# Output weights of the second layer split one stage earlier and held in DRAM, and squares added up by VectorE after a transpose

## The chip, the cores and the metric

The kernel runs on one core of a Trainium2 chip. Its five engines are TensorE (PE in the profile; PEld is its weight load), VectorE (DVE), ScalarE (ACT), GpSimd (POOL) and SyncE (SP, which only issues DMAs here). The metric is device time in microseconds (us): the median of the runs of one program, 617.97 us for the kernel before (3 runs, 617.78 to 618.43).

## The reference

An encoder of two layers works on 256 positions of width 1024. A layer is a mixer and a feed-forward:

```python
h = rms_norm(x, n1); proj = h @ w_in_l                 # 1024 -> 2560
# q, k, v of three groups of heads (width 64): 4 neighbourhood, 6 dilated, 6 grouped-query heads
mix = concatenate([rms_norm(out_a, og[:256]), rms_norm(out_d, og[256:640]), rms_norm(out_c, og[640:])])
x = x + mix @ w_out_l                                  # 1024 -> 1024
h = rms_norm(x, n2); g, u = split(h @ w_gu, 2)         # 1024 -> 2 x 2816
x = x + (gelu(conv(g)) * u) @ w_dn                     # 2816 -> 1024
```

Everything is float32. Each of the three groups of heads has a norm of its own ahead of the output projection: the squares of a group's outputs are added over the group's width, position by position.

## The kernel before

**Arithmetic.** A float32 product is made of three fast ones. Each weight is split into a high part, rounded to the type float32r, and a low part, the rest; each activation likewise. `mm3` (L610) multiplies high by high, high by low and low by high.

**Weights** come in units (`units_of`, L544). A layer has 51: 12 of the projection w_in, 6 of w_out (L70: two halves of columns for each of three groups; four units of 3 x 512 columns per partition and two of 2 x 512), 11 each of gate, up and down. `load` (L561) issues one DMA per unit on SP's queue into one of four raw tiles. `split` (L584) makes the two parts in chunks, mostly of 512 columns: ScalarE copies to the high part, VectorE subtracts that from the raw values for the low part. There are two high and two low tiles, so a unit's split can begin only when the matmuls of the unit two before are done. `unit` (L599) takes the next unit and asks for the splits and loads ahead of it.

**The mixer** of a layer (L789 to L1225) normalises and transposes x, projects, and then runs 16 heads in the order dilated, grouped-query, neighbourhood: scores, softmax, transpose of the probabilities, product with the values. `Weave` (L665) puts the matmuls of the projections, and then those of the first four output units (`out_projections`, L826), between the steps of the heads. For each pair of heads `mixed` (L1032) writes the two parts of the outputs into `mixT_hi` and `mixT_lo`, and has the squares made on ScalarE and added on GpSimd. When a group's heads are done, `group_rstd` (L1047) adds those squares over the partitions: on TensorE, two matmuls of the squares with a column of ones, each of which the chip executes as two; VectorE copies the two result columns, and GpSimd works out the factor (`rstd_of`, L615: two instructions). The output projection's sum is then scaled by that factor and added to x on VectorE (L842). After the last group, the fifth and the sixth output unit remain (L1221 to L1225). x is transposed in two halves for the feed-forward (`split_T`, L623), the second of them between the gate unit's matmuls (L1249).

**The feed-forward** has 11 steps. Each takes a gate unit and an up unit (`half_up`, L1234) and a down unit (`down`, L1308). In steps 2 to 4 of layer 0 some tables for layer 1 are made (L1323 to L1330).

**Order.** Nothing is issued as it is written. `Plan` (L220) records every operation with an estimated duration (`cost`, L414), and `order` (L301) lists them again: always the one next that can start first by these estimates, and among equals the one of the lowest rank. `later(n)` adds n to the rank. `emit` (L406) then issues each in this order, so that nearly all instructions have line L411 in the profile and are told apart by their tiles: `wp_raw`, `wp_hi` and `wp_lo` are weights, `act_hT` is the transposed normalised x, `act_mixT` are the heads' outputs, `act_sqm` their squares, `const_x` is x, `psa` and `psw` are PSUM. Every engine then executes its list strictly in order.

Of the kernel before, what the change touches and what calls it, by code (L numbers as in the profile page):

```python
# [29 lines left out]
DEPTH = 2  # L30
# [6 lines left out]
UNIT = 2048  # L37
# [4 lines left out]
RAWS, PARTS, AHEAD, CHUNK = 4, 2, 2, 512  # L42
# [10 lines left out]

SUM_ACT, SCALE_ACT = ("dq", "dk", "cq"), ("dk",)

SPLIT_LATER, TURN_LATER, MIX_LATER, PREP_LATER = 50, 100, 100, 30
GKV_W = H_GKV * HD
_CD = 3 * H_NA * HD
_WD = H_DIL * HD
# [10 lines left out]
OUT_ORDER = [(0, 0), (0, 512), (1, 0), (1, 512), (2, 0), (2, 512)]  # L70

FFN = [("G", 0), ("U", 0)]
# [147 lines left out]
class Plan:  # L220
# [5 lines left out]
    def pool(self, real, name, bufs, space=bass.MemoryType.SB):  # L226
        return PlanPool(self, real, name, bufs, space)
# [226 lines left out]
def encoder_kernel(  # L454
# [21 lines left out]
    nc = Plan(tc)  # L476
# [3 lines left out]
    const = pool("const", 1)  # L480
    wp = pool("wp", 3)
    act = pool("act", 2)
# [3 lines left out]
    dram = pool("dram", 1, space=bass.MemoryType.DRAM)  # L486
# [7 lines left out]
    ident = const.tile([P, P], F32, tag="ident", name="ident")  # L494
# [7 lines left out]
    def load_x(c, n, by):  # L502
        cs = slice(c * P, (c + n) * P)
        by.dma_start(xs[:, :, cs], xv[:, :, cs])
# [23 lines left out]
    minus_half = const.tile([P, 32], F32, tag="mh", name="minus_half")  # L528
    nc.gpsimd.memset(minus_half, -0.5)

    ones = const.tile([P, 1], F32, tag="ones", name="ones")
    nc.gpsimd.memset(ones, 1.0)

    vown, vkv = (
        [const.tile([P, NT, 2 * n + 1, HD], F32R, tag=f"v{n}{i}", name=f"v{n}{i}") for i in range(2)]
# [8 lines left out]
    def units_of(l):  # L544

        for c0, width in PROJ:
            per = 4 if width * 8 > UNIT else 8
            for k0 in range(0, KD, per):
                yield rows(w_in[l], k0, per, c0, width)
        for gi, c0 in OUT_ORDER:  # L550
            yield rows(w_out[l], *OUTP[gi], c0, 512)
        for kind, s in FFN:
            if kind == "D":
                yield rows(w_down[l], 2 * s, 2, 0, D)
            else:
                yield rows(w_gate_up[l], 0, KD, (D_FF if kind == "U" else 0) + s * 2 * P, 2 * P)

    views = [v for l in range(DEPTH) for v in units_of(l)]
    raws, parts, taken = [], [], [0]

    def load(i):  # L561
        v = views[i]
        a, b = v.shape[1], v.shape[2]
        raw = wp.tile([P, UNIT], F32, tag="raw", name=f"raw{i}", bufs=RAWS)
        rv = raw[:, : a * b].rearrange("p (a b) -> p a b", b=b)
        if i == 0:
            for by, what, c in START:
                by = nc.scalar if by == "act" else nc.sync
                if what == "w":
                    by.dma_start(rv[:, c], v[:, c])  # L570
                elif what == "x":
                    load_x(*c, by)
                elif what == "ident":
                    by.dma_start(ident, c_ident)
                elif what == "g":
                    by.dma_start(gl0 if c == 0 else gl1[16 * c - 16 : 16 * c], gsrc[c])
            nc.first_loads = len(nc.ops)
        else:
            for c in range(0, a, 2 if i == 1 else a):
                e = c + 2 if i == 1 else a  # L580
                nc.sync.dma_start(rv[:, c:e], v[:, c:e])
        raws.append(raw)

    def split(i):  # L584
        v = views[i]
        a, b = v.shape[1], v.shape[2]
        n = a * b
        raw = raws[i]
        hi = wp.tile([P, UNIT], F32R, tag="hi", name=f"hi{i}", bufs=PARTS)
        lo = wp.tile([P, UNIT], F32R, tag="lo", name=f"lo{i}", bufs=PARTS)  # L590
        h = b if i < 2 else b * max(1, CHUNK // b)
        for c in range(0, n, h):
            e = min(c + h, n)
            nc.scalar.copy(hi[:, c:e], raw[:, c:e])
            nc.vector.tensor_tensor(lo[:, c:e], raw[:, c:e], hi[:, c:e].bitcast(F32), op=ALU.subtract)
        r = lambda z: z[:, :n].rearrange("p (a b) -> p a b", b=b)
        parts.append((r(hi), r(lo)))
# [150 lines left out]
    def tables_d(l, which):  # L748
        cd = act.tile([P, NT, HD], F32, tag=f"cd{which}", name=f"cd{which}{l}", bufs=1)
        sd = act.tile([P, NT, 16], F32, tag=f"sd{which}", name=f"sd{which}{l}", bufs=1)  # L750
        b = lambda v: v.unsqueeze(1).to_broadcast([P, NT, v.shape[1]])
        nc.gpsimd.tensor_tensor(cd, gains_of["rot"][:, :, 0:64], b(gains_of[which][:, l, 1]), op=ALU.mult)
        for i in range(2):
            o, n = (8 * i, 8 * (1 - i)), 8
            nc.gpsimd.tensor_tensor(
                sd[:, :, o[0] : o[0] + n],
                gains_of["rot"][:, :, 64 + o[0] : 64 + o[0] + n],
                b(gains_of[which][:, l, 1, o[1] : o[1] + n]),
                op=ALU.mult,
            )  # L760
        return cd, sd
# [21 lines left out]
    def tables_of(l):  # L783
        for which in "qk":
            tables["d" + which, l] = tables_d(l, which)
        for which in "qk":
            tables["c" + which, l] = tables_c(l, which)

    load(0)  # L789
    for l in range(DEPTH):  # L790

# [255 lines left out]
        def group_rstd(gi):  # L1047

            _, n = OUTP[gi]
            ps = psw.tile([P, 512], F32, tag="w", name=f"gs{gi}{l}")  # L1050
            for t in range(NT):
                nc.tensor.matmul(
                    ps[:, t : t + 1], hold["sq", gi][:, t * P : (t + 1) * P], ones, start=True, stop=True
                )
            ss = small.tile([P, NT], F32, tag="ss2", name=f"ss_m{gi}{l}")
            nc.vector.tensor_copy(ss, ps[:, :NT])
            group_r[gi] = rstd_of(ss, NT, n * P, EPS, f"m{gi}{l}")
            wv.give(f"mix{gi}")


        hold, turned = {}, {}
# [262 lines left out]
        for kind, s in FFN:  # L1324
            if kind == "G" and l + 1 < DEPTH and s in NA_STEPS:
                with nc.not_before("SP"):
                    NA_STEPS[s](l + 1)
            if kind == "G" and l + 1 < DEPTH and s == 4:
                with nc.not_before("POOL"):
                    tables_of(l + 1)  # L1330
            if kind == "G":
                gate(s)
            elif kind == "U":
                up(s)
            elif s < STEPS - 2:
                down([s])
            else:
                last.append(s)
# [80 lines left out]
```

## Time and profile before

| | |
|---|---|
| median of 3 runs | 617.97 us |
| the profiled execution | 617.81 us, of which the span of the trace 616.0 us |
| granted TensorE clock | 0.999 |
| feed-forward of layer 0 | from about 129 to 311 us |
| mixer of layer 1 | from about 311 to 430 us |
| DMA | 104.66 MB, mean 170 GB/s |

A time in the profile counts from the span's start. A row of the timeline gives the start, the busy time, the engine, the line, the operation with the tile it writes and those it reads, the shapes, the count of instructions that were merged, and in brackets the idle time before, with what ended it. A row of a group gives the count, the busy us, the mean ns of one, the idle time before and what ended it. The rows that matter here are quoted in the prediction.

### The profile page before, as it was taken

Reading aid. Unit: us, or ns where it says so; the run is one execution under the profiler, and the core shown is the slowest. Engines: PE = TensorE matmul, PEld = TensorE weight load, DVE = VectorE, ACT = ScalarE, POOL = GpSimd, SP = SyncE. Lnnn points to the kernel's source line nnn. Section 1 sums busy time; section 2 is a strip of 40 time slices with the busy share of each in tenths; the row PEclk is TensorE's granted clock in tenths of the full one; section 3 lists DMA queues with packets and bytes.
Section 4 is the critical chain, followed back from the end, with each engine's and each line's share of the span. In section 5 each row is a group of like instructions: output and inputs, shape, how many; then the busy total and the mean of one; then the engine's idle time right before and its main releaser. Section 6 shows DMA issues by size and latency. Waiting matters only on the chain.

```text
span 616.0 us, 9844 instructions
## 1 busy us (share of the span) xinstructions
PE 606.0 (98%) x3496; PEld 524.8 (85%) x3496; DVE 485.8 (79%) x1000; ACT 428.8 (70%) x1064; POOL 77.4 (13%) x125
## 2 busy tenths in 40 slices
PE   8999999999999999999999999999999999999997
PEld 6999878888888888888899989887888888888886
DVE  4898988897877877777867798979877777777775
ACT  6888989686566565556588899897756565566551
POOL 2731230211500000000023212112000000000000
PEclk9999999999999999999999999999999999999999
DMA  8894311755596555655444632127575555555501
GB/s 284 274 291 146 103 38 37 245 195 197 183 231 222 178 197 204 199 169 162 155 148 150 233 104 86 34 73 243 182 238 173 191 205 186 169 192 204 168 40 68
DMA packets 81617, 104.66 MB, mean 170 GB/s; under 512 B 9480, under 2 KB 69224, under 8 KB 81568
## 3 DMA queue, kind: packets, MB, share of 16 engines
q1 hardware_dynamic: 81024, 103.78, 52.0%
q8 instruction: 27, 0.44, 0.3%
q10 hardware_dynamic: 544, 0.26, 0.1%
q14 instruction: 22, 0.18, 0.1%
HBM read 102.54 MB, written 1.49 MB: 169 GB/s over the span
## 4 chain that ended last, share of the span: by engine, by line
PE 93%; ACT 3%; DVE 2%; DMA 1%; issue 1%; SPq 0%; ACTq 0%; DVEq 0%
PE psw_w L411 49%; PE psa_a L411 44%; ACT act_s2k L411 2%; DMA wp_raw<-in_w_in_dram 1%; DVE act_hT L411 1%; DVE wp_lo L411 1%; DVE const_x L411 0%; ACT wp_hi L411 0%; ACT act_hT L411 0%; ACT act_ch L411 0%; SPq L411 0%; DVE act_cl L411 0%; DVE act_z L411 0%; ACT const_v L411 0%; DVE small_nm L411 0%
## 5 line engine op out<-in xcount | busy, mean ns | idle before, releaser
L411 DVE TENSOR_TENSOR wp_lo<-wp_raw,wp_hi 128x512 fp32r<-128x512 f32 (+2 forms) x348 | 243.9, 729 | 49.7 <-ACT wp_hi L411 47.8
L411 PE MATMUL psw_w<-act_hT,wp_hi 128*128 128x512 f32 x704 | 247.6, 397 | 2.0 <-DVE act_hT L411 2.0
L411 ACT CAST wp_hi<-wp_raw 128x512 fp32r<-128x512 f32 (+2 forms) x348 | 212.7, 660 | 29.3 <-PE psw_w L411 15.6
L411 PE MATMUL psw_w<-act_hT,wp_lo 128*128 128x256 f32 x704 | 195.7, 279 | 0.0
L411 PEld LDWEIGHTS psw_w<-act_hT,wp_hi 128*128 128x128 f32 x704 | 131.8, 188 | 34.1 <-DVE act_hT L411 3.2
L411 PEld LDWEIGHTS psw_w<-act_hT,wp_lo 128*128 128x128 f32 x704 | 132.6, 188 | 1.2
L411 PE MATMUL psa_a<-wp_hi,act_hT 128*128 128x384 f32 (+2 forms) x448 | 113.1, 333 | 1.3 <-ACT act_hT L411 1.2
L411 ACT COPY act_s2k<-psw_w 128x256 f32<-128x256 f32 x88 | 32.3, 372 | 80.2 <-PE psw_w L411 80.2
L411 PEld LDWEIGHTS psa_a<-wp_hi,act_hT 128*128 128x128 f32 x448 | 77.9, 189 | 4.5 <-ACT act_hT L411 1.6
L411 PE MATMUL psa_a<-wp_lo,act_hT 128*128 128x384 f32 (+2 forms) x224 | 74.6, 334 | 0.0
L411 PE MATMUL psa_a<-wp_lo,act_ch 128*128 128x512 f32 x176 | 69.5, 395 | 0.0
L411 PE MATMUL psa_a<-wp_hi,act_ch 128*128 128x512 f32 x176 | 69.3, 394 | 0.0
L411 PE MATMUL psa_a<-wp_hi,act_cl 128*128 128x512 f32 x176 | 66.1, 394 | 0.0
L411 DVE TENSOR_TENSOR act_s2k<-psw_w,act_s2k 128x256 f32<-128x256 f32 x88 | 36.8, 422 | 32.4 <-ACT act_s2k L411 31.9
L411 PEld LDWEIGHTS psa_a<-wp_lo,act_hT 128*128 128x128 f32 x224 | 42.2, 189 | 1.9 <-DVE wp_lo L411 1.0
L411 PEld LDWEIGHTS psa_a<-wp_hi,act_cl 128*128 128x128 f32 x176 | 33.2, 188 | 7.7
L411 PEld LDWEIGHTS psa_a<-wp_hi,act_ch 128*128 128x128 f32 x176 | 33.1, 188 | 7.8
L411 PEld LDWEIGHTS psa_a<-wp_lo,act_ch 128*128 128x128 f32 x176 | 33.1, 188 | 6.9
L411 DVE SCALAR_TENSOR_TENSOR act_s2k<-act_s2k,act_cw,act_s2k 128x255 f32<-128x255 f32 x88 | 36.7, 476 | 1.4 <-ACT act_s2k L411 1.3
L411 POOL TENSOR_TENSOR small_rstd<-small_ms,const_mh 128x6 f32<-128x6 f32 (+2 forms) x26 | 32.0, 1232 | 2.2
L411 ACT ACTIVATE act_s2k<-act_s2k,act_cw 128x256 f32<-128x256 f32 x44 | 24.1, 595 | 11.6 <-DVE act_s2k L411 11.6
L411 PE MATMUL psw_w<-act_ch,const_v 128*128 128x256 f32 x128 | 28.5, 287 | 1.6 <-ACT act_s2k L411 1.1
(109 smaller groups left out, 754.3 us busy)
## 6 DMA issues: line engine op xcount, KB each, us to landing
wp_raw<-in_w_gate_up_dram SPq DMA_DIRECT2D x44, 1024.0 KB, 5.0
wp_raw<-in_w_down_dram SPq DMA_DIRECT2D x22, 1024.0 KB, 4.8
wp_raw<-in_w_in_dram SPq DMA_DIRECT2D x14, 768.0 KB, 5.9
wp_raw<-in_w_in_dram SPq DMA_DIRECT2D x8, 1024.0 KB, 5.9
wp_raw<-in_w_out_dram SPq DMA_DIRECT2D x8, 768.0 KB, 4.3
wp_raw<-in_w_out_dram SPq DMA_DIRECT2D x4, 512.0 KB, 3.8
act_nab<-dram_scr SPq DMA_DIRECT2D x4, 448.0 KB, 7.0
out_dram<-const_x SPq DMA_DIRECT2D x4, 256.0 KB, 2.0
```

Source lines behind the costliest of these rows:

```text
L411: getattr(o.engine.real, o.method)(*map(real, o.args), **{k: real(v) for k, v in o.kw.items()})
```

## The change

**Output weights.** In each of the steps 4 to 9 of layer 0's feed-forward, `keep` loads one output unit of layer 1 into a raw tile, has it split (ScalarE and VectorE, chunks of 512) into tiles that share their place with `mixT_hi` and `mixT_lo`, which are free in that stage, and stores the two parts into DRAM by two DMAs on SP's queue. When the unit's turn comes in layer 1, `load` does nothing and `split` fetches both parts from DRAM into the high and the low tile by two DMAs that GpSimd issues.

**Squares.** In `group_rstd` the squares are transposed (two transposes with the identity), and VectorE adds up each row of the result, in both layers and all three groups. The column of ones is gone.

```diff
-SPLIT_LATER, TURN_LATER, MIX_LATER, PREP_LATER = 50, 100, 100, 30
+SPLIT_LATER, TURN_LATER, MIX_LATER, PREP_LATER, KEEP_LATER = 50, 100, 100, 30, 100
+KEEP_STEPS = range(4, 10)
...
+    def keep(i):
+        v = views[i]
+        a, b = v.shape[1], v.shape[2]
+        n = a * b
+        raw = wp.tile([P, UNIT], F32, tag="raw", name=f"raw{i}", bufs=RAWS)
+        nc.sync.dma_start(raw[:, :n].rearrange("p (a b) -> p a b", b=b), v)
+        hi, lo = (act.tile([P, UNIT], F32R, tag=f"mixT_{g}", name=f"k{g}{i}", bufs=1) for g in ("hi", "lo"))
+        with nc.later(KEEP_LATER):
+            for c in range(0, n, CHUNK):
+                e = c + CHUNK
+                nc.scalar.copy(hi[:, c:e], raw[:, c:e])
+                nc.vector.tensor_tensor(lo[:, c:e], raw[:, c:e], hi[:, c:e].bitcast(F32), op=ALU.subtract)
+            kept[i] = [dram.tile([P, n], F32, tag=f"k{g}{i}", name=f"k{g}{i}") for g in ("hi", "lo")]
+            for d, z in zip(kept[i], (hi, lo)):
+                nc.sync.dma_start(d, z[:, :n].bitcast(F32))
...
     def load(i):
         v = views[i]
+        if i in kept:
+            raws.append(None)
+            return
...
     def split(i):
...
-        for c in range(0, n, h):
+        if i in kept:
+            for d, z in zip(kept[i], (hi, lo)):
+                nc.gpsimd.dma_start(z[:, :n], d)
+        for c in range(0, n if i not in kept else 0, h):
...
             for t in range(NT):
-                nc.tensor.matmul(
-                    ps[:, t : t + 1], hold["sq", gi][:, t * P : (t + 1) * P], ones, start=True, stop=True
-                )
+                cols = slice(t * P, (t + 1) * P)
+                nc.tensor.transpose(ps[:, cols], hold["sq", gi][:, cols], ident)
             ss = small.tile([P, NT], F32, tag="ss2", name=f"ss_m{gi}{l}")
-            nc.vector.tensor_copy(ss, ps[:, :NT])
+            nc.vector.reduce_sum(ss, ps[:, :S].rearrange("p (t d) -> p t d", d=P), axis=AX.X)
...
+            if kind == "G" and l + 1 < DEPTH and s in KEEP_STEPS:
+                keep((l + 1) * PER_LAYER + LAST_OUT - len(OUT_ORDER) + s - KEEP_STEPS[0])
```

What the changed program's lists show: TensorE has as many instructions as before. In the mixer of layer 1 the heads' last matmul stands earlier among those of the output units, and at its end the eight transposes of x's first half stand before all matmuls of the sixth output unit, where five of that unit's matmuls stood before the first of them. On GpSimd the twelve DMAs stand in pairs between the additions of squares and the group factors; the last pair stands just before the two instructions of the last group's factor.

More of the change, by code (lines that the diff above doesn't have):

```diff
@@ L529, in encoder_kernel @@
     nc.gpsimd.memset(minus_half, -0.5)
-    ones = const.tile([P, 1], F32, tag="ones", name="ones")
-    nc.gpsimd.memset(ones, 1.0)
     vown, vkv = (
@@ L559, in encoder_kernel @@
     raws, parts, taken = [], [], [0]
+    PER_LAYER = len(views) // DEPTH
+    LAST_OUT = PER_LAYER - len(FFN)
+    kept = {}
+    def keep(i):
[13 more added lines that the diff above has]
+                nc.sync.dma_start(d, z[:, :n].bitcast(F32))
     def load(i):
         v = views[i]
+        if i in kept:
+            raws.append(None)
+            return
         a, b = v.shape[1], v.shape[2]
```

## The prediction

> **What bounds the kernel now.** I read the page first, then busy time by stretch, then the chain of waits, and then TensorE's own waits in the stretch that the change relieves.
>
> ```profile
> span 616.0 us, 9844 instructions
> ...
> PE 606.0 (98%) x3496; PEld 524.8 (85%) x3496; DVE 485.8 (79%) x1000; ACT 428.8 (70%) x1064; POOL 77.4 (13%) x125
> ...
> PE 93%; ACT 3%; DVE 2%; DMA 1%; issue 1%; SPq 0%; ACTq 0%; DVEq 0%
> ```
>
> TensorE is busy 98% of the span and makes 93% of the chain that ended last. Here is what the other engines do beside it in the feed-forward of layer 0, in the mixer of layer 1 and in the feed-forward of layer 1.
>
> ```profile
> 128.70:311.00 182.30, 182.26 (x954) 154.94 (x955) 141.97 (x240) 111.64 (x204) 10.84 (x19) 1.00 0.62 196
> 311.00:430.50 119.50, 117.99 (x781) 105.89 (x779) 101.09 (x262) 104.10 (x333) 26.69 (x38) 1.00 0.39 129
> 430.50:612.40 181.90, 181.88 (x954) 154.61 (x954) 136.67 (x231) 106.94 (x193) 0.04 (x1) 1.00 0.50 169
> ```
>
> The columns are the length, then busy us of PE, PEld, DVE, ACT and POOL, the granted clock, the DMA share and GB/s. In the mixer of layer 1 DVE is busy 85% and ACT 87%, in the feed-forward of layer 0 they are at 78% and 61%. So work moved from the one to the other moves to where there is room. But in that mixer TensorE is idle only 1.51 us out of 119.50 (119.50 - 117.99). A busy matmul may hide a short wait, because matmuls overlap; the pace has to be looked at too.
>
> ```profile
> 143.33 5.56 PE psa_a L411 x24
> 148.90 11.29 PE psw_w L411 x64
> ```
>
> These two pieces of the chain are one down unit and a gate and an up unit without a stall: 24 matmuls of 512 columns in 5.56 us, so 0.232 us each, and 0.116 us for one of 256. Against that pace I look at the weight loads that came late in the mixer of layer 1 (a late load shows a wait that the busy matmuls cover), and at TensorE's open idle time there:
>
> ```profile
> PEld psw_w L411 <- DVE act_hT L411: 2.0, 2, 1.6
> PEld psw_w L411 <- issue: 0.7, 3, 0.3
> PEld psw_w L411 <- ACT act_ch L411: 0.6, 1, 0.6
> PEld psa_a L411 <- DVE wp_lo L411: 0.5, 2, 0.3
> PEld psw_w L411 <- DVE act_cl L411: 0.4, 1, 0.4
> PEld psa_a L411 <- ACT act_mixT_hi L411: 0.3, 1, 0.3
> PEld psw_w L411 <- ACT wp_hi L411: 0.2, 1, 0.2
> PEld psw_w L411 <- DVE act_z L411: 0.2, 1, 0.2
> PEld psa_a L411 <- DVE act_z L411: 0.2, 1, 0.2
> ```
>
> That is the whole room for relief: 2.4 us of small waits for ACT and DVE (0.6 + 0.5 + 0.4 + 0.3 + 0.2 + 0.2 + 0.2), and 2.0 us before the feed-forward, which have another cause (below). However much ACT and DVE are freed, no more than some 4.4 us can come back here.
>
> **Part 1: the splits leave the mixer.** The six output units of layer 1 are four of 1536 columns and two of 1024, so 16 chunks of 512. In that stretch, a group of DVE and one of ACT, with the mean ns of one:
>
> ```profile
> L411 DVE TENSOR_TENSOR wp_lo<-wp_raw,wp_hi 128x512 fp32r<-128x512 f32 x39 | 25.3, 684 | 2.2 <-ACT wp_hi L411 2.1
> L411 ACT CAST wp_hi<-wp_raw 128x512 fp32r<-128x512 f32 x40 | 22.9, 629 | 3.2 <-issue 2.0 <-PE psa_a L411 1.1
> ```
>
> 16 x 0.684 = 10.9 us of DVE and 16 x 0.629 = 10.1 us of ACT leave. They were beside matmuls, so what counts is the late loads above. Bounds are 0 and -2.4 us; as the order of the changed kernel puts the last attention matmul some 3.5 us of matmul work earlier, I take half, **-1.2 us**.
>
> **Part 2: the splits arrive in the feed-forward of layer 0**, one unit in each of the steps 4 to 9. One step, from one such stretch:
>
> ```profile
> 212.20:228.90 16.70, 16.70 (x89) 14.21 (x88) 12.37 (x22) 9.82 (x19) 0.00 (x0) 1.00 0.57 188
> ```
>
> DVE goes from 12.37 to 12.37 + 3 x 0.684 = 14.4 us of 16.70, ACT from 9.82 to 11.7. TensorE stays the slowest, and it does not wait for them today. The DMAs: 0.79 MB of raw weights (loaded in the mixer before) and 2 x 0.79 MB of stores per step, 2.36 MB in 16.7 us or 141 GB/s on top of 188. By the share at hand (0.57 for 188) that would be 1.0; the pieces are 2 KB and 6 KB rows where most of today's are of 1 KB, so I expect 0.85 to 0.95. The two stores stand on SP's queue and wait for ACT's and DVE's split; the weight loads behind them wait too. What covers it: a raw tile is loaded when the split four units before has freed its slot, and split three units (3 x 5.56 us) later. With a fourth unit per step in the ring this falls to about two units, 11 us, against the landing of about 5 us. So I take **0**, with 0 to +3 us as bounds; without that cover each late load would stall TensorE by its whole delay.
>
> **Part 3: the loads in the mixer of layer 1 move to POOL's queue.** Twelve of them, high and low part of each unit, wait until the matmuls on the slot's old unit are done. POOL runs in order, so behind each pair stand the additions of squares and the group norms' factors, and for the last of these the whole end of the mixer waits. No row here shows a DMA issued by POOL. The rows nearest to its cost in POOL's time (call it D), and to its landing:
>
> ```profile
> L411 SPq DMA_DIRECT2D wp_raw<-in_w_out_dram x12: 367/368/368, 43.1 to 396.1; - x12
> ...
> 417.98 0.74 POOL L411 TENSOR_TENSOR act_sqm<-act_sqm,act_sqm 128x256 f32<-128x256 f32 x1 [5.48 <-ACT act_sqm L411]
> ...
> L411 POOL COPY act_nab<-act_few x2: 1831/1833/1835, 24.2 to 151.9; 28x1984 f32<-28x1984 f32 x2
> ...
> wp_raw<-in_w_out_dram SPq DMA_DIRECT2D x8, 768.0 KB, 4.3
> wp_raw<-in_w_out_dram SPq DMA_DIRECT2D x4, 512.0 KB, 3.8
> ```
>
> D lies between SP's 0.37 us for the same transfer and the 1.83 us of POOL's longest copy; I take 0.74, one POOL instruction over 128 partitions. How long each unit may take, counted from the changed kernel's matmul order at the pace above (from the last matmul of the slot's old unit to the first of the new): 8.6, 7.8 and 8.9 us for the second to fourth unit, 5.8 for the fifth, 4.0 for the sixth. Needed are 0.2 for the handover, D, and the second load's landing behind the first: with 4.3 us, and about 1 us for the first one's bytes, 6.2 us for a big pair, and with 3.8 us and 0.7 5.4 us for a small pair. So the first five fit, and the sixth doesn't.
>
> The end of the mixer before, row by row:
>
> ```profile
> 419.05 0.50 PE L411 MATMUL psw_w<-const_ones,act_sqm 128*128 128x1 f32 x4
> 419.41 0.27 PE L411 MATMUL psw_w<-const_ident,act_s2k 88*128 88x88 f32 x1
> 419.59 0.16 DVE L411 COPY small_ss<-psw_w 128x2 f32<-128x2 f32 x1
> 419.83 0.19 POOL L411 TENSOR_SCALAR small_ms<-small_ss 128x2 f32<-128x2 f32 x1 [1.11 <-DVE small_ss L411]
> 420.11 1.03 POOL L411 TENSOR_TENSOR small_rstd<-small_ms,const_mh 128x2 f32<-128x2 f32 x1
> 421.17 1.41 DVE L411 SCALAR_TENSOR_TENSOR const_x<-psa_a,small_rstd,const_x 128x512 f32<-128x512 f32 x2
> 423.26 0.82 PE L411 MATMUL psw_w<-const_ident,const_x 128*128 128x128 f32 x6
> 423.84 0.47 PE L411 MATMUL psa_a<-wp_lo,act_mixT_hi 128*128 128x512 f32 x1
> 425.20 0.50 PE L411 MATMUL psw_w<-act_hT,wp_hi 128*128 128x512 f32 x1
> 430.48 0.50 PE L411 MATMUL psw_w<-act_hT,wp_hi 128*128 128x512 f32 x1 [1.34 <-DVE act_hT L411]
> ...
> 411.80 0.71 POOL L411 TENSOR_TENSOR small_rstd<-small_ms,const_mh 128x2 f32<-128x2 f32 x1
> ```
>
> Call 419.05 T; the fourth unit's matmuls end there. Today TensorE goes on through the fifth and sixth unit, with the transposes of x in between, and the factor (ready at T + 2.1) is in time. In the changed order the eight transposes of x stand before the sixth unit's matmuls, and POOL has the sixth unit's two loads, which wait for T, before the factor. So: handover 0.2, two issues 1.48, POOL free at T + 1.7. The factor's two instructions take 0.28 + 0.71 (the 0.71 of 411.80 and not the 1.03 of 420.11, since no subtraction of weights stands beside it on DVE in the new order): T + 2.7. Two updates of x, 1.41: T + 4.2, with the handover 4.4. TensorE has 0.3 us of transposes and 12 x 0.232 = 2.8 us of the fifth unit, so it is there at T + 3.1 and waits **+1.3 us**. The transposes take 0.8, to T + 5.2; the sixth unit, by then 0.2 + 5.2 after T, is just in time. The wait of 1.34 us at 430.48 stays: in both orders five subtractions of weights stand on DVE between the last update of x and the second half of h (0, bounds -0.4 and +0.3).
>
> [...]
>
> **Part 4: squares.** Six times, four weight loads and matmuls with a column of ones (419.05 to 419.41: 0.36 us) become two transposes (423.26 to 423.84: six in 0.58, so 0.1 us each): -0.16 us each, all on TensorE's path, **-1.0 us**. Bounds -1.4 and -0.4. DVE reads 256 columns in place of 2:
>
> ```profile
> L411 DVE TENSOR_REDUCE small_nm<-psw_w 128x1 f32<-128x256 f32 x12 | 4.4, 415 | 0.7 <-PE psw_w L411 0.6
> ```
>
> so 0.42 in place of the 0.16 of 419.59. Nobody waits for four of the six; in the mixer of layer 0 the last stands on the path to x: **+0.2 us** (0 to 0.3). In layer 1 POOL is behind anyway.
>
> **The sum**: -1.2 + 0 + 1.3 - 1.0 + 0.2 = -0.7. The profiled execution took 617.8 us (1.8 around its span), close to the median of 617.97, so **617.1 us**: within 0.2% of before (616.7 to 619.2), which is about what a measurement of this kernel can tell from no change.
>
> **The rivals.**
> (a) *POOL's issues are dear: slower.* The sum grows by 2 us per us of D over 0.74 through the factor, and from D = 0.9 by another 2 through the fifth unit, which then lands late. It is zero at D = 1.05 and 0.2% slower at D = 1.5. With 1.83 it is +2.2 for the factor, +1.9 for the fifth unit and 0.6 for the second and third: 621.8 us. If the transfers themselves are slow (they copy float32 into a float32r tile, which no row shows), all five intervals fail, at a price of some 4 us each, 635 us. For it: POOL's order, and intervals with no cover. Against: 13% busy POOL.
> (b) *The relief is larger, faster.* All late loads and half of the 2.0 us vanish, and the wait at the end is covered, since the factor's squares are ready earlier: -2.4 - 1.0 - 1.0 + 0.2 = -4.2, and 0 to 1 us for the end: 614.2 us. For it: ACT at 87% and DVE at 85%, and attention ending 3.5 us of work earlier. Against: a TensorE that is idle 1.51 us.
> (c) *The feed-forward of layer 0 overflows*: DMA at a share of 1, SP's queue stopped behind stores. If a load is late by 1 us per step in six steps: 617.1 + 4 to 6, 622 us. Against: some 6 us of slack per load, no wait of TensorE there now.
> (d) *It doesn't do what it says.* The order of the changed kernel shows the 16 casts and 16 subtractions in the feed-forward; excluded.
>
> **How the numbers follow.** Forecast (615.6 to 618.8) 0.45, of which 0.17 below 616.7 and 0.26 within 0.2%; (a) 0.26; (b) 0.22; (c) 0.07. Faster by over 0.2%: 0.17 + 0.22 = 0.39. Within: 0.26. Slower: 0.02 + 0.26 + 0.07 = 0.35. The range of 613.8 to 623.5 takes in (b), (a) up to D = 1.83 with no relief, and most of (c); slow transfers stay out. The forecast's own range is 615.6 to 618.8.
>
> **What would show it.** TensorE's waits in the feed-forward of layer 0 stay at none, with DMA at 0.85 to 0.95 in steps 4 to 7 (part 2). The late loads of the mixer fall from 2.4 to about 1.2 us (part 1). POOL's DMA instructions show D. At the end of that mixer TensorE waits 1.3 us for an update of x before the eight transposes (part 3); if it waits for a landing of the weights' parts instead, or for one in the units before, (a) is right. The transposed squares take 0.2 us each (part 4). Wrong would be a time over 619.2 with D below 1, or under 616 with late loads unchanged.

## The result and the profile after

The changed kernel takes 617.3 us (median of 20 runs, 616.39 to 617.99) against 618.19 us (20 runs) for the kernel before: a ratio of 0.9986, 95% interval 0.998 to 0.9993, so 0.9 us or 0.14% less. The profiled execution has a span of 615.5 us. Its page, the rows that answer to those of before:

```profile
span 615.5 us, 9869 instructions
...
PE 604.9 (98%) x3484; PEld 523.7 (85%) x3484; DVE 486.9 (79%) x1000; ACT 428.3 (70%) x1064; POOL 84.0 (14%) x136
```

Busy time by stretch (length, busy us of PE, PEld, DVE, ACT, POOL, granted clock, DMA share, GB/s): the feed-forward of layer 0, the mixer of layer 1, and two of the stretches with stores, the first and the fourth:

```profile
127.50:309.80 182.30, 182.09 (x955) 154.98 (x956) 150.22 (x256) 119.00 (x220) 9.70 (x19) 1.00 0.80 264
309.80:429.07 119.27, 116.99 (x774) 105.34 (x772) 92.56 (x246) 96.51 (x317) 33.34 (x50) 1.00 0.49 165
...
195.00:211.50 16.50, 16.50 (x89) 13.98 (x87) 15.96 (x28) 10.47 (x21) 0.00 (x0) 1.00 1.02 364
...
245.00:262.00 17.00, 17.00 (x91) 14.51 (x90) 14.43 (x26) 11.27 (x22) 0.00 (x0) 1.00 0.92 318
```

The work has moved as meant: DVE falls from 101.09 to 92.56 us in the mixer of layer 1, ACT from 104.10 to 96.51 (8.5 and 7.6 us, where the sum counted 10.9 and 10.1), and in the feed-forward TensorE has no gap (16.50 of 16.50) though the DMA engines are full. Yet TensorE is idle 2.28 us in that mixer (119.27 - 116.99), where it was idle 1.51 us.

To see where the 0.9 us went I take four rows that both kernels have: ScalarE's first pass over the neighbourhood projection of layer 0, the first GELU of layer 0, the last update of x in layer 0 and the first GELU of layer 1. The kernel before:

```profile
77.93 1.11 ACT L411 ACTIVATE act_s2k<-psa_a 128x512 f32<-128x512 f32 x2
...
138.78 0.63 ACT L411 ACTIVATE act_s2k<-act_s2k 128x512 f32<-128x512 f32 x1
...
311.22 0.75 DVE L411 SCALAR_TENSOR_TENSOR const_x<-psa_a,small_rx,const_x 128x512 f32<-128x512 f32 x1 [0.65 <-PE psa_a L411]
...
440.51 0.63 ACT L411 ACTIVATE act_s2k<-act_s2k 128x512 f32<-128x512 f32 x1
```

And after:

```profile
77.70 1.10 ACT L413 ACTIVATE act_s2k<-psa_a 128x512 f32<-128x512 f32 x2
...
137.76 0.63 ACT L413 ACTIVATE act_s2k<-act_s2k 128x512 f32<-128x512 f32 x1
...
309.93 0.75 DVE L413 SCALAR_TENSOR_TENSOR const_x<-psa_a,small_rx,const_x 128x512 f32<-128x512 f32 x1 [0.65 <-PE psa_a L413]
...
439.12 0.63 ACT L413 ACTIVATE act_s2k<-act_s2k 128x512 f32<-128x512 f32 x1
```

The first interval, the heads of layer 0, shrinks from 60.85 to 60.06 us (-0.79). The second, the feed-forward of layer 0, from 172.44 to 172.17 (-0.27), which is within what single executions differ by (below). The third, the mixer of layer 1, for which the change was made in the main, from 129.29 to 129.19 (-0.10). So the gain stands in **layer 0's mixer**, where the prediction had -0.3, and not in layer 1's, where it had -0.4 (-1.2 + 1.3 - 0.5). The stretches before the first row and after the last one are not part of this: they were -0.23 and +0.89 us in this pair of executions, and they vary by half a microsecond and more between executions of the same lists. The two mixers together, -0.89 us, are what the medians show.

In the mixer of layer 1 the late weight loads of TensorE (engine and tile that waited, what for, us in total, times, longest) are now:

```profile
PEld psw_w L413 <- DVE act_hT L413: 1.4, 1, 1.4
PEld psw_w L413 <- DVE const_x L413: 1.1, 2, 0.7
PEld psw_w L413 <- ACT act_s2k L413: 0.8, 1, 0.8
PEld psw_w L413 <- issue: 0.7, 3, 0.3
PEld psw_w L413 <- DVE wp_lo L413: 0.4, 1, 0.4
PEld psa_a L413 <- DVE wp_lo L413: 0.3, 1, 0.3
PEld psw_w L413 <- ACT wp_hi L413: 0.2, 1, 0.2
```

Together 4.9 us, against 5.1 before. The waits for `act_ch`, `act_cl`, `act_mixT_hi` and `act_z` are gone (1.7 us), but there are new ones: 1.1 us for x, which the prediction had, and 0.8 us for probabilities (`act_s2k`), which it had not.

The end of that mixer, by the timeline (start, busy us, engine, operation, in brackets the idle time before):

```profile
415.68 0.57 POOL L413 DMA_DIRECT2D wp_lo<-dram_klo  x1 [1.72 <-PE psa_a L413]
...
416.14 0.38 PE L413 MATMUL psw_w<-const_ident,act_sqm 128*128 128x128 f32 x2
416.25 0.54 POOL L413 DMA_DIRECT2D wp_hi<-dram_khi  x1
...
417.01 0.41 DVE L413 TENSOR_REDUCE small_ss<-psw_w 128x2 f32<-128x256 f32 x1
...
417.52 0.19 POOL L413 TENSOR_SCALAR small_ms<-small_ss 128x2 f32<-128x2 f32 x1 [0.73 <-DVE small_ss L413]
417.79 0.71 POOL L413 TENSOR_TENSOR small_rstd<-small_ms,const_mh 128x2 f32<-128x2 f32 x1
...
418.54 0.75 DVE L413 SCALAR_TENSOR_TENSOR const_x<-psa_a,small_rstd,const_x 128x512 f32<-128x512 f32 x1 [0.96 <-POOL small_rstd L413]
...
420.26 0.87 PE L413 MATMUL psw_w<-const_ident,const_x 128*128 128x128 f32 x6 [0.48 <-DVE const_x L413]
...
429.07 0.50 PE L413 MATMUL psw_w<-act_hT,wp_hi 128*128 128x512 f32 x1 [1.13 <-DVE act_hT L413]
```

Each of the last two issues takes GpSimd 0.54 to 0.57 us. The last pair is done at 416.79, and then GpSimd **waits 0.73 us** for the sum of squares. So the issues aren't on the way to the factor.

### The profile page after: what moved, and what is told of

It reads as the page before. It is cut to its first block, busy times and chain, and to the rows that moved or that the text cites. A ratio compares the mean times of both kernels' runs of the same rounds, so it can differ in the third digit from the quotient of the medians.

```text
span 615.5 us, 9869 instructions
## 1 busy us (share of the span) xinstructions
PE 604.9 (98%) x3484; PEld 523.7 (85%) x3484; DVE 486.9 (79%) x1000; ACT 428.3 (70%) x1064; POOL 84.0 (14%) x136
## 4 chain that ended last, share of the span: by engine, by line
PE 92%; DVE 3%; ACT 2%; issue 1%; DMA 1%; POOL 0%; SPq 0%; DVEq 0%; ACTq 0%
PE psw_w L413 49%; PE psa_a L413 43%; DVE const_x L413 1%; ACT act_s2k L413 1%; DVE wp_lo L413 1%; DMA wp_raw<-in_w_in_dram 1%; DVE act_hT L413 1%; ACT act_hT L413 1%; ACT wp_hi L413 1%; POOL small_rstd L413 0%; ACT act_mixT_hi L413 0%; POOL small_ms L413 0%; SPq L413 0%; DVE act_mixT_lo L413 0%; DVE small_ss L413 0%
## 5 line engine op out<-in xcount | busy, mean ns | idle before, releaser
L413 DVE TENSOR_TENSOR wp_lo<-wp_raw,wp_hi 128x512 fp32r<-128x512 f32 (+2 forms) x332 | 232.3, 731 | 42.9 <-ACT wp_hi L413 41.4
L413 ACT CAST wp_hi<-wp_raw 128x512 fp32r<-128x512 f32 (+2 forms) x332 | 203.1, 662 | 26.1 <-PE psw_w L413 15.3
```

Of the source, the lines that this page charges most:

```text
L413: getattr(o.engine.real, o.method)(*map(real, o.args), **{k: real(v) for k, v in o.kw.items()})
```

## The experiments

All kernels, with the length of the two mixers in their profiled execution, measured between the rows above, as a difference from before. The change's own line is the first. Each ratio is to the kernel before as it was timed beside that run (medians of 617.8 to 618.2 us). The feed-forwards are left out: that of layer 1 took 171.90 or 172.44 us in eleven of the thirteen profiled executions, and kernels with the very same lists (before_new_order and squares_only, below) had one and the other, so half a microsecond there belongs to the execution. That of layer 0 took 171.8 to 172.5 us in all but stores_twice. Each mixer was profiled once per kernel.

| kernel | median us | ratio to before (95%) | mixer of layer 0 | mixer of layer 1 |
|---|---|---|---|---|
| the change | 617.3 | 0.9986 (0.998 to 0.9993) | -0.79 | -0.10 |
| squares_only | 619.5 | 1.0026 (1.0016 to 1.0037) | -0.79 | +3.22 |
| keep_only | 618.44 | 1.0008 (0.9999 to 1.0017) | 0.00 | +0.49 |
| keep_four | 615.78 | 0.9961 (0.9948 to 0.9973) | -0.80 | -1.12 |
| loads_on_sp | 616.83 | 0.9978 (0.9969 to 0.9987) | -0.81 | -0.15 |
| squares_old_order | 617.86 | 0.9998 (0.9989 to 1.0006) | -0.02 | +0.41 |
| before_new_order | 618.66 | 1.0008 (0.9999 to 1.0017) | -0.71 | +1.54 |
| fetch_in_four | 619.85 | 1.0033 (1.002 to 1.0045) | -0.80 | +2.18 |
| fetch_early_plan | 616.18 | 0.9972 (0.9961 to 0.9984) | -0.79 | -0.69 |
| relief_only | 617.47 | 0.9996 (0.9987 to 1.0005) | 0.00 | -0.26 |
| stores_twice | 626.73 | 1.0145 (1.0129 to 1.016) | -0.82 | -0.24 |
| high_part_first | 616.58 | 0.9978 (0.997 to 0.9987) | -0.79 | -1.09 |

In squares_only's profiled execution the granted TensorE clock was 0.53 over 3.6 us at the end of layer 1's mixer; by an estimate from that, some 1.7 of its 3.22 us are the clock (last section).

**1. The two halves apart.** squares_only is the kernel before with the three lines of `group_rstd` changed; keep_only is the changed kernel with the column of ones put back.

> The kernel before, with the squares of the group norms transposed and added up by VectorE, and nothing else. Theory A (the prediction's steps): -1.0 + 0.2 = -0.8 us, a ratio to before of 0.9987; that is -0.3 in the mixer of layer 0 and -0.5 in that of layer 1. Theory B (from the two traces: the changed kernel's matmuls run 0.2 us ahead of those before at 78 us, 1.1 us ahead at 120 us, and no more than 1.3 us ahead anywhere later): the squares and the new order that they bring in the mixer of layer 0 are the whole gain, so -0.9 to -1.1 us, ratio 0.998 to 0.9986, with about -0.9 in the mixer of layer 0. If the ratio is 0.9995 or more, both fall, and the splits' move brought the gain.

> The change without its squares: six output units of layer 1 split in the feed-forward of layer 0, fetched by GpSimd, sums by the column of ones as before. Theory A (relief of 1.2 us in the mixer of layer 1, less the 0.65 us wait that the trace after shows at its end): -0.55 us, ratio 0.9991. Theory B (new waits eat the relief): 0, ratio 0.9995 to 1.0008, with the matmuls as far ahead at the start of layer 1's mixer as at its end.

Measured: squares_only 1.0026, *slower* by 1.4 us; keep_only 1.0008. Theory A falls for both. Theory B is right on layer 0's mixer (-0.79) and on keep_only, and wrong on squares_only as a whole. Alone, the squares lose and the kept units gain nothing (the interval of keep_only holds 1); together they gain. In keep_only's mixer of layer 1 TensorE is idle 1.6 us for h, 0.6 for x and 0.6 for probabilities, where it was idle 1.3 for h and 0.2 for the parts of the probabilities: new waits for the old ones. So the parts cannot be priced one by one. Either half makes `Plan.order` list the instructions anew.

**2. Order or work.** In squares_old_order the plan is told the old durations for the squares' operations, in before_new_order the durations of the new ones for the old operations:

```diff
+            nc.hint = 1.04 * NT + 70          # squares_old_order; 1.04 * S + 70 in before_new_order
             nc.vector.reduce_sum(ss, ...)     # the copy in before_new_order
+            nc.hint = None
```

> The squares alone, as in squares_only, but the plan is told the old durations for them, so that every engine has the list of the kernel before with nothing but the two transposes and the sum by VectorE in the place of the matmuls with ones and the copy. Theory C (what squares_only lost, it lost by the new order of the plan, not by the work): 6 x -0.16 + 0.2 = -0.8 us, ratio to before 0.9987 (0.998 to 0.9993), and TensorE's waits in the mixer of layer 1 are those of before. Theory D (the sum over 256 columns on VectorE is itself what delays the end of the mixers): slower than before like squares_only, ratio 1.002 or more.

> The kernel before, with the matmuls with ones and the copies as they were, but the plan is told the durations of the new squares, so that every engine has the list of squares_only. Theory C (order): slower than squares_only by the squares' own 0.8 us, ratio to before 1.0035 (1.002 to 1.005), with the long waits of squares_only at the end of layer 1's mixer (for the probabilities, for x, for the parts of h). Theory D (work): as before, 0.9995 to 1.0005.

Measured: 0.9998 and 1.0008. In **layer 0** theory C holds fully: the new list gives -0.71 us with the old work, and the new work -0.02 with the old list. The gain of the change there is one of order: in that stretch TensorE, ScalarE and VectorE of the changed kernel have their work in the order of before_new_order. The late loads at 95 to 131 us show it, first before, then before_new_order:

```profile
PEld psw_w L411 <- DVE act_hT L411: 1.2, 2, 0.9
PEld psw_w L411 <- ACT act_ch L411: 0.6, 1, 0.6
PEld psw_w L411 <- DVE act_cl L411: 0.3, 1, 0.3
...
```

```profile
PEld psw_w L414 <- DVE act_hT L414: 1.5, 2, 1.3
...
```

The waits for the parts of the probabilities (0.6 and 0.3) are gone and 0.3 is given back at h. In **layer 1** the same new list costs +1.54 us, without any new work. As a whole before_new_order misses theory C, which had it 0.8 us slower than squares_only: it is some 0.8 us faster, 0.6 us over before where squares_only is 1.4 over. The lower clock of squares_only's profiled execution does not explain that: its five runs with a mean clock of 0.999 or 1.0 (619.2 to 619.8 us) are slower than before_new_order's 618.66 too, and why the new squares cost with the new list isn't shown. Nor does the old list with the new work gain the predicted 0.8 us: 0.9998 says -0.2 us, with the interval between -0.7 and +0.4, and in layer 1 the mixer is 0.41 longer. Its end, in squares_old_order:

```profile
419.03 0.42 DVE L414 TENSOR_REDUCE small_ss<-psw_w 128x2 f32<-128x256 f32 x1
...
419.52 1.29 DVE L414 TENSOR_TENSOR wp_lo<-wp_raw,wp_hi 128x512 fp32r<-128x512 f32 x2
...
419.54 0.72 POOL L414 TENSOR_SCALAR small_ms<-small_ss 128x2 f32<-128x2 f32 x1 [1.36 <-DVE small_ss L414]
420.34 1.03 POOL L414 TENSOR_TENSOR small_rstd<-small_ms,const_mh 128x2 f32<-128x2 f32 x1
...
421.40 1.41 DVE L414 SCALAR_TENSOR_TENSOR const_x<-psa_a,small_rstd,const_x 128x512 f32<-128x512 f32 x2 [0.60 <-POOL small_rstd L414]
```

The sum takes 0.42 us in place of 0.16, and this pushes GpSimd's first instruction from just ahead of VectorE's two subtractions of weights to just behind their start: it takes 0.72 us and not the 0.19 of before. Counted from the last update of x in layer 0 (311.22 before, 310.69 here), the sum starts as early as the copy did (108.34 us for 108.37), and the update of x 0.76 us later (110.71 for 109.95). That is the 0.26 + 0.53 = 0.79 us of these two instructions. In layer 0 TensorE is 0.43 us ahead at its last squares, and that is lost on the same way to x. In the changed kernel's layer 1 the output units' subtractions are gone from that place, and the two GpSimd instructions take 0.19 and 0.71 us: 0.85 us that the one half saves for the other. That doesn't decide the total, though: in keep_four (below) the subtractions are back there, the two take 0.72 and 1.03 us (1.96 us from the end of its sum at 417.69 to the update of x at 419.65), and that kernel is faster.

Why GpSimd takes longer there isn't shown. What the rows show is 0.72 us for the first instruction where it starts beside the subtractions (419.54 here) against 0.19 without them (417.52 in the change), and 1.03 against 0.71 us for the second.

**3. GpSimd's issues.** loads_on_sp lets SyncE issue the fetches, all other lists as in the changed kernel; fetch_in_four splits each fetch in four:

```diff
-                nc.gpsimd.dma_start(z[:, :n], d)
+                nc.sync.dma_start(z[:, :n].bitcast(F32), d)      # loads_on_sp
```

> The changed kernel with the twelve fetches issued by SyncE in place of GpSimd, and without a change of type (the tile is addressed as float32). Theory A: GpSimd is free of two issues ahead of the factor, so -0.65 us (the whole wait before the transposes of x) against the changed kernel, ratio to before 0.9975. Theory B (the issues were hidden behind the addition of the squares): 0 to -0.2 us against the changed kernel, ratio 0.9982 to 0.9987. A third way: the fetches wait in SyncE's queue for their slots with the raw loads of the feed-forward behind them, and those come late: slower than before, by a microsecond or more, with TensorE waiting for splits at the start of the feed-forward of layer 1.

> The changed kernel with each fetch issued as four DMAs over a quarter of the columns, and the same lists on all engines otherwise. If an issue costs GpSimd 0.55 us whatever its size, the last pair takes 4.4 us in place of 1.1. Theory A (the prediction's slope, all of GpSimd's time before the last factor counts): +3.3 us there, and more where other pairs stand before additions of squares: ratio to the changed kernel 1.005 or more. Theory B (issues are covered by the transposes and the addition of the squares, to 1.75 us after the slot is free): +2.65 us, the wait before the transposes of x grows from 0.65 to 3.3 us; ratio to before 1.0025 to 1.0045. If an issue costs in proportion to its size, nothing changes and the ratio is that of the changed kernel, 0.998 to 0.9993.

Measured: loads_on_sp 0.9978, the mixer of layer 1 as long as in the changed kernel (-0.15 for -0.10), and TensorE waits there for x 0.49 us (0.48 in the change). The ratio alone doesn't decide, as it is nearer to theory A's 0.9975 and its interval takes in both; that wait, which theory A would have gone, is theory B. The medians of the two, 0.5 us apart, have intervals that overlap. fetch_in_four is 1.0033, its mixer 2.28 us longer than the change's. Its GpSimd at the same place:

```profile
415.65 0.57 POOL L416 DMA_DIRECT2D wp_lo<-dram_klo  x1 [1.03 <-PE psa_a L416]
416.43 2.11 POOL L416 DMA_DIRECT2D wp_hi<-dram_khi  x4 [0.21 <-PE psa_a L416]
418.51 1.62 POOL L416 DMA_DIRECT2D wp_lo<-dram_klo  x3
420.20 0.19 POOL L416 TENSOR_SCALAR small_ms<-small_ss 128x2 f32<-128x2 f32 x1
```

A quarter of a fetch (128 KB) takes 0.53 us (2.11 / 4), as much as a whole one of 512 KB (0.54 to 0.57 in the change): here the price is per DMA and not per byte. The factor's first instruction starts at 420.20 in place of 417.52, so 2.68 us later; theory B said 2.65. In the changed kernel the sum of squares is ready at 417.42 and the slot free at 415.68, so, as an estimate from these rows, two issues are covered up to D = 0.87 us ((417.42 - 415.68) / 2), and every microsecond of D over that costs two.

**4. The last two units, and the last few instructions.**

> The changed kernel with only the first four output units of layer 1 kept; the fifth and sixth are loaded and split in the mixer as before, so no DMA of GpSimd stands ahead of the last group's factor. Theory A (the last pair's issues are on the way to the factor, as the prediction has it): the factor comes two issues, 1.1 us, earlier, the wait of 0.65 us before the transposes of x goes, four of sixteen chunks of split come back (+0.3): -0.35 us against the changed kernel, ratio to before about 0.998. Theory B (the issues end 0.7 us before VectorE has added the squares up, so nobody waits for them): the factor comes as late as before, and the time is that of the changed kernel within 0.3 us, or up to 0.5 us more for the splits on VectorE between the updates of x, ratio 0.9985 to 0.9995.

> The changed kernel with the same work; the plan is told that GpSimd's fetches land 1.8 us earlier. All lists are the same up to the end of layer 1's mixer; there, two transposes of x, then two matmuls of the sixth output unit, and then the other six transposes stand where eight transposes stood, and four subtractions of weights in place of five stand before the second half of h. Theory C (the order of these few instructions decides): the waits at the mixer's end fall from 2.3 us to about 1.1 as in keep_four, so -1.0 to -1.2 us against the changed kernel, ratio to before 0.9960 to 0.9972. Theory E (keep_four gained by not keeping the last two units): no change against the changed kernel, 0.998 to 0.9993.

keep_four (`KEEP_STEPS = range(4, 8)`) gains 0.9961, more than either theory said: it is 2.3 us faster than before. But not because GpSimd is free sooner: the factor's first instruction stands behind the sum of squares in both. fetch_early_plan keeps all six and only tells the plan that fetches land earlier:

```diff
-                end = max(end + 900, wires.get(ring, 0.0))
+                end = max(end + (0 if e == "POOL" else 900), wires.get(ring, 0.0))
...
-                end = wires[ring] + 900
+                end = wires[ring] + (0 if e == "POOL" else 900)
```

It comes to 0.9972, 1.1 us under the change's median, with the same work; its mixer of layer 1 is 0.59 us shorter than the change's (keep_four's 1.02). Theory C, at the edge of what it named; whether a part of keep_four's gain is its own isn't settled, as the intervals of the two overlap. The list has traded waits: for x 0.4 in place of 1.1 us, for h 0.7 in place of 1.4, but now TensorE waits for a landing. In fetch_early_plan:

```profile
PEld psa_a L413 <- DMA wp_hi<-dram_khi: 1.3, 1, 1.3
...
PEld psw_w L413 <- DVE act_hT L413: 0.7, 1, 0.7
```

high_part_first follows that 1.3 us. It changes the order of the three products in the fourth and the sixth unit of layer 1, so that the high part is fetched first:

```diff
+        if low_last:
+            nc.tensor.matmul(ps, al, bh, start=False, stop=False)
+            nc.tensor.matmul(ps, ah, bl, start=False, stop=last)
+            return
```

> fetch_early_plan with another order of the three products in the fourth and the sixth output unit of layer 1 alone: high by high, low activations by high weights, high activations by low weights. So the high part's slot is free first, its fetch is issued first, and the low part is needed last. Theory H (in fetch_early_plan TensorE waits 1.26 us for the landing of the sixth unit's high part, which is issued second): the wait falls to 0.3 us or less, -0.8 to -1.0 us against fetch_early_plan, ratio to before 0.9955 to 0.9962. Rival: the time only moves to the next wait, that for the second half of h (0.59 us in fetch_early_plan, which grows by as much), ratio 0.9968 to 0.9976.

Measured 0.9978: no gain over fetch_early_plan (0.9972), and so not theory H. Nor does the rival hold as it was put, since the wait for h did not grow. In the trace the mixer is 0.40 us shorter, which the runs don't bear out, and which of the two is right stays open. The wait for the landing is cut in two:

```profile
420.69 0.47 PE L413 MATMUL psa_a<-wp_hi,act_mixT_hi 128*128 128x512 f32 x1 [0.51 <-DMA wp_hi<-dram_khi]
...
421.85 0.50 PE L413 MATMUL psa_a<-wp_lo,act_mixT_hi 128*128 128x512 f32 x1 [0.24 <-DMA wp_lo<-dram_klo]
...
429.05 0.50 PE L413 MATMUL psw_w<-act_hT,wp_hi 128*128 128x512 f32 x1 [0.27 <-DVE act_hT L413]
```

**5. The relief by itself.** relief_only is the kernel before with its lists, but each chunk of the six output units is cast and subtracted in 8 of its 512 columns:

```diff
+            if out_unit:
+                e = c + 8
             nc.scalar.copy(hi[:, c:e], raw[:, c:e])
```

> The kernel before with the same lists on all engines (the plan is told the old durations), but of each chunk of 512 columns of the six output units of layer 1 only 8 columns are cast and subtracted; the rest of the parts is left as the unit two before left it, so the output projection of layer 1 is not the reference's. ScalarE and VectorE are rid of some 20 us of work in the mixer of layer 1, and nothing else changes. Theory A (the prediction's part 1): -1.2 us, bounds 0 and -2.4, ratio 0.998 (0.9961 to 1). Theory F (in the changed kernel the relief is no more than the waits of TensorE that went there: 0.32, 0.14, 0.14 and 0.12 us, 0.7 in all): -0.7 us, and some 0.3 more if GpSimd's factor gets quicker without subtractions beside it, ratio 0.9984 to 0.999.

Measured: 0.9996, so -0.3 us with bounds of -0.8 and +0.3; the mixer of layer 1 is 0.26 us shorter. Theory A's -1.2 falls, though -0.3 lies within its bounds of 0 and -2.4, and F is at the edge. In that mixer VectorE is busy 7.9 us less and ScalarE 6.0 us less, nearly the relief of the change, and TensorE's waits for the heads are still there:

```profile
...
PEld psw_w L414 <- DVE act_cl L414: 0.6, 2, 0.4
PEld psw_w L414 <- ACT act_ch L414: 0.6, 1, 0.6
...
```

The longest of them, for `act_ch`, ends behind this copy on ScalarE:

```profile
406.45 0.60 PE L414 MATMUL psw_w<-const_ident,act_s2k 128*128 128x128 f32 x4
...
408.68 0.56 ACT L414 CAST act_ch<-psw_w 128x512 fp32r<-128x512 f32 x1
```

What the copy reads was there by 407.05. But from 406.88 on ScalarE works without a gap through the softmax of other heads, which stands ahead of the copy in its list; no weight split is among it. One of the two waits for `act_cl` (0.37 us at 391.12) has mostly another cause, the length of a chain: the transposes end at 389.29, the copy starts at 389.33, and the subtraction follows it at 390.14, 0.2 us after the copy's end. Neither wait is shorter than in the kernel before (0.59 and 0.37 us there): what the splits leave free is not what they waited for. That another list can end such waits is shown for layer 0 (experiment 2).

**6. The stores.**

> The changed kernel with each store of the parts in the feed-forward of layer 0 issued twice (the second one to a place that nobody reads), all other lists the same. 1.57 MB more per step of 16.7 us; the steps with stores move 318 to 364 GB/s at a share of 0.92 to 1.02 as it is, so 4.3 us of transfers per step no longer fit. Theory A (the prediction's part 2: the stores are covered by some 6 us of slack per load, and cost the whole delay beyond it): after two steps the slack is used up, loads of weights come late and TensorE waits for splits, +4 to +10 us, ratio to before 1.005 to 1.015. Theory G (a share near 1 is no limit, or the stores are not in the way of loads): no change against the changed kernel, ratio 0.998 to 0.9993.

Measured: 1.0145, +8.9 us; theory A. A stall, the stretch after it, and the instruction that caused it:

```profile
207.50:212.50 5.00, 2.19 (x13) 1.63 (x11) 0.32 (x2) 0.68 (x2) 0.00 (x0) 1.00 1.07 364
212.50:217.00 4.50, 3.99 (x11) 3.16 (x12) 4.50 (x8) 4.50 (x10) 0.00 (x0) 0.62 1.06 404
```

```profile
211.82 0.62 ACT L416 CAST act_mixT_hi<-wp_raw 128x512 fp32r<-128x512 f32 x1 [4.55 <-DMA wp_raw<-in_w_out_dram]
```

The first load to come late is not one of the feed-forward's, as theory A had it, but that of the next kept unit, which stands behind the stores in SyncE's queue. Its cast stands on ScalarE ahead of a cast of the activations, and TensorE waits for that. It does so twice, for 5.7 us in all; and beside each wait the granted clock is down (0.62 over 4.5 us here, 0.69 over 5.0 us around the second), which by these figures is an estimated 3 us more. So the change as it is has its transfers within what the stage can take, and doubled stores do not fit.

## Why the prediction was right in the time, and where its steps failed

The time, 617.3 for 617.1, is right; the way to it is in good part not, and that the two agree so closely is luck. Step by step:

- **Part 2, the feed-forward of layer 0: right.** No wait of TensorE, DMA at 0.92 to 1.02 in place of the 0.85 to 0.95 expected. That larger pieces would lower the share was the author's estimate: per 100 GB/s it is 0.28 and 0.29 (1.02 for 364, 0.92 for 318) where it was 0.30 (0.57 for 188). stores_twice shows what a late load costs where the transfers no longer fit.
- **Part 1, the relief: wrong.** "I take half, -1.2 us": by itself it is -0.3 (relief_only, -0.8 to +0.3). The step that failed is to count every wait for ACT and DVE as one for the splits: without them these waits fall only from 2.4 to 2.1 us, and those for `act_ch` and `act_cl` not at all (1.0 before, 1.2 in relief_only). In the changed kernel these two did go, under another list, and 0.8 us for probabilities came in their place: by the prediction's own count the small waits fall from 2.4 to 1.7 us, not to 1.2.
- **Part 3, the end of the mixer: the wait is there and has the right releaser, but its size and reason are off.** Predicted 1.3 us, measured 0.48 of idle TensorE (1.1 us of late loads). D was 0.55 and not 0.74, but that isn't it: the sum put the two issues behind T, while the slot was free 0.46 us before T (415.68 for 416.14) and the transposes, the sum of squares and their handovers last longer than the issues. With that x is ready at T + 4.1 and not T + 4.4; and two of the eight transposes run before that, between the two updates of x, where the sum had all eight behind both. So the sixth unit starts at T + 4.75 and not at T + 5.2. The slope "2 us per us of D" holds, by the estimate above, only from D = 0.87 on (the rows of the change; fetch_in_four agrees). No landing was late, as the sum had it; its 1 and 0.7 us for the bytes of a pair's first fetch were estimates without a row, and the high part, mostly the second, took 1.3 us (768 KB) and 0.7 us (512 KB) longer from issue to landing than the low one. "The wait of 1.34 us stays" is right: 1.13 us idle, behind five subtractions.
- **Part 4, the squares: the matmuls right, the chain wrong.** In layer 0 TensorE is 0.43 us ahead where the third group's squares begin (squares_old_order), where the sum had 2 x 0.16 = 0.32. But the +0.2 us for the way to x should have been 0.5 there and 0.8 in layer 1, where the later sum puts GpSimd beside VectorE's subtractions. "POOL is behind anyway" was the wrong sentence.
- **Not in the sum at all: the plan's new list in the mixer of layer 0**, -0.71 us (before_new_order). It is the largest single term of the result. I had compared the lists for layer 1 only.

Predicted for layer 0's mixer -0.3, measured -0.79; for layer 1's -0.4, measured -0.10. The two errors, -0.5 and +0.3, go against each other. Of the rivals, (a) is out by D, and (c) as TensorE had no wait in that feed-forward; (b) named 614.2 for a relief that relief_only does not show, though a kernel of 615.78 exists (keep_four). One figure of (a) is off: by its own slopes a time 0.2% above before is reached at D = 1.35 and not at 1.5. Nothing hangs on it, with D at 0.55.

What stays open: why the changed list has the new 0.8 us wait for probabilities at 383 us (all kernels with kept units have it, none other; no kernel here changes that alone), why the new squares cost with the new list in layer 1 (squares_only against before_new_order), and how much of keep_four's lead over fetch_early_plan is real.

## What to carry to other kernels

Where a planner orders the instructions by estimated durations, an edit of any operation is two edits, and the second, the new list, can be the larger: run the new work with the old list and the old work with the new one before you credit either. A wait of the bounding engine for a busy engine is relieved by moving work only if the work moved stands right ahead of the awaited instruction in that engine's list (in relief_only 7.9 us less of VectorE and 6.0 us less of ScalarE came to 0.3 us); look at what the engine did in the microseconds before the wait ended, and at when the chain was started. An issue on the path is free as long as something else on that path is slower (here GpSimd waits 0.73 us behind two issues of 1.11 us), so price it from where the other branch ends, not from zero.

## What the runs showed of the hardware

**A granted clock of 0.53 after a pause of 1.60 us.** In squares_only's profiled execution TensorE pauses 1.60 us before a matmul at 426.37, in a stretch with little work (0.80 us busy of 2.40), and the granted clock falls to 0.53 over the next 3.6 us (the columns are those of the stretches above):

```profile
424.00:426.40 2.40, 0.80 (x7) 0.57 (x7) 2.33 (x5) 2.40 (x7) 0.00 (x0) 1.00 0.76 300
426.40:430.00 3.60, 3.60 (x11) 3.08 (x12) 3.60 (x8) 2.89 (x8) 1.85 (x3) 0.53 0.07 7
```

before_new_order, with the same list, pauses 1.55 us at the same place and keeps its clock:

```profile
426.40:430.00 3.60, 3.60 (x24) 3.12 (x23) 3.60 (x8) 2.98 (x8) 1.85 (x3) 1.00 0.09 18
```

11 matmuls against 24 in the same 3.6 us: at a clock of 0.53 TensorE loses an estimated 1.7 us (3.6 x 0.47), which is the difference between the two mixers of layer 1 in the table (3.22 and 1.54). It doesn't hit each execution: those of squares_only with a mean clock of 0.999 or 1.0 took 619.2 to 619.8 us, those with 0.997 took 620.2 and 621.0. In the profiled execution the pause and the clock behind it come to an estimated 3.3 us (1.60 + 1.7), twice the pause. That this pause is the cause is inferred from its place; one trace shows it. In stores_twice the clock is at 0.62 and 0.69 beside waits of 3.3 and 2.4 us; in fetch_in_four TensorE pauses 1.94 us before a matmul at 422.03, and the mean clock of that execution is 1.0. From which length on a pause costs clock isn't shown.

**A fetch that GpSimd issues** (operation, count, KB each, median us from issue to landing), in the changed kernel:

```profile
wp_lo<-dram_klo POOLq DMA_DIRECT2D x4, 768.0 KB, 4.8
...
wp_lo<-dram_klo POOLq DMA_DIRECT2D x2, 512.0 KB, 3.8
```

SyncE's issues of the same transfers land after 4.3 and 3.8 us (loads_on_sp). The high part, mostly the second of a pair, takes 6.1 and 4.5 us by GpSimd and 5.9 and 4.6 by SyncE. So here issuing by GpSimd, with the change of type, costs 0.5 us or less in landing (4.8 for 4.3, 3.8 for 3.8, 6.1 for 5.9, 4.5 for 4.6), and 0.54 to 0.79 us of GpSimd's own time for each fetch.
